# Products with V moved out of the delta-rule recurrence of a hybrid decoder step

## The chip, the core and the metric

The kernel runs on one core of a Trainium2 chip. The metric is device time in microseconds of one execution, the median of the runs. Engines: PE (TensorE) multiplies, PEld is its weight load, DVE (VectorE) and ACT (ScalarE) work elementwise, POOL (GpSimd) too, SP issues DMAs. Each engine takes its instructions in the order in which the program holds them.

## What is computed

One layer over 1024 prompt tokens and 8 x 8 sample tokens, all in float32, D_MODEL 1024. An input projection feeds a short gated convolution and an RWKV-7 head group (8 heads of 64); an output projection, a residual, a squared-ReLU MLP of 4096 and norms follow. The part that the change touches is the state recurrence of each head:

```
def step(s, inp):
    r_t, w_t, k_t, v_t, kk_t, a_t = inp
    s_kk = einsum('bhvk,bhk->bhv', s, kk_t)
    s = s * w_t[:, :, None, :] - s_kk[..., None] * (kk_t * a_t)[:, :, None, :] + v_t[..., None] * k_t[:, :, None, :]
    y_t = einsum('bhvk,bhk->bhv', s, r_t)
    return s, y_t
```

## The kernel before, in words

**Matrix products that fill.** The projections are cut into pieces of 24 matmuls (`fill`, lines L664 and L671, tile `acc`), each matmul 128 x 128 weights against 384, 320 or 256 columns, in the float32r format, three passes over high and low parts. They depend on little and are called fillers here.

**The recurrence.** It runs over chunks of 64 tokens. Heads go in pairs p = 0..3 (head 0 of a pair on partitions 0 to 63, head 1 on 64 to 127), tokens in groups g = 0..2. A unit u = 3p + g has 6, 6 or 4 prompt chunks (64 chunks in all), and the unit g = 2 has one more chunk with the sample tokens (`gen_sample`). For each unit `gen_norms` and `gen_ew` make scaled keys, `gen_tokens` transposes keys and values (KT, VT), masked products land in AMK and AMB (L899, tile `pm`), `gen_invert` solves a 32 x 32 triangular inverse on POOL, `gen_merge` completes it to 64 x 64 on PE (tile `pz`). Then `gen_recur` does per chunk, into one PSUM bank `rc`: KT x V (L1110), AMK x V (L1111), AR x state (L1114), copy to X (L1120, DVE), Tt x X (L1122), scale to UT (L1124, ACT), KT x UT (L1126), and the new state Gh (L1132, DVE), which takes in GD, the decayed old state (L1116, ACT). The weights of these products are 128 x 128, block-diagonal over the two heads, with zeros in the other blocks. The outputs `py` (L1144) are 64 x 64 products, two heads side by side. `gen_finish` normalises py, transposes it (tile `pty`) and gates it.

**What sets the order.** The whole front of the kernel is written by generators; a planner (`Weave.run`) takes from them, one at a time, the step that could start first by its own table of costs, and so writes out the order of every engine once, at build time. A step may need credits (`acq`): PSUM banks by tag (`mm`, `tr`, `rec`, `iv`, `py`), buffers for r, k and v (`xr`, `xk`, `xv`, three each). A filler piece whose result finds no free buffer holds its `mm` bank, and the fillers behind it stand. The order of the projection jobs is the list `main`. After the front, the MLP loop runs in plain program order; the change does not touch it.

Of the kernel before, what the change touches and what calls it, by code (L numbers as in the profile page):

```python
# [28 lines left out]
REC, TR = 2, 2  # L29
# [4 lines left out]
def tile_kernel(ctx: ExitStack, tc: tile.TileContext, io: dict):  # L34
# [227 lines left out]
    class Weave:  # L262
# [47 lines left out]
        def run(self, gens):  # L310

            st = [[0.0, next(g, None), "PE"] for g in gens]
            while any(a is not None for _, a, _ in st):
# [37 lines left out]
                st[i][0] = r if o.get("nb") else t + cost + o.get("lat", self.LAT[eng])  # L351
# [147 lines left out]
    def gen_lora(parts):  # L499

        for p in range(4):
            for g in range(3):
                s, n = GROUPS[g]
                pc = slice(128 * p, 128 * p + 128)
                for nm in parts:
                    x, dst = {"w2": (lw, sig_d), "a2": (la, ta_d), "g2": (None, gate_d)}[nm]
                    m = 3 if x is None else 2
                    yield ck("PE", (n / 2400 + 0.0133) * m, acq=("rec",),
                             deps=[("lw", nm), ("sg" if x is None else "la", g)])
                    pw = ps.tile([128, 512], F32, tag="rec", name="pw", bufs=REC)  # L510
# [12 lines left out]
                    wv.free("rec")  # L523
# [208 lines left out]
    def first(g):  # L732
# [4 lines left out]
    main = (rkv_jobs(0) + conv_jobs(0, "cxb") + conv_jobs(1, "cxb") + rkv_jobs(1) + conv_jobs(2, "cx") + rkv_jobs(2)  # L737
            + conv_jobs(2, "b") + rkv_jobs(3) + conv_jobs(3, "cxb"))
# [4 lines left out]
    def gen_open():  # L743
# [14 lines left out]
        for nm, w, n in (("AR", 192, 3), ("AMK", 192, 3), ("KT", 256, 2)):  # L758
            at[nm + "s"] = [pp.tile([128, 6, w], F32, name=f"{nm}{i}") for i in range(n)]
        load_sgta(0)  # L760
        load_gt(0)
        for i in range(3):
            for h in range(2):
                r, z = slice(64 * h, 64 * h + 64), slice(64 - 64 * h, 128 - 64 * h)
                G.memset(at["ARs"][i][r, :, z], 0.0)
                G.memset(at["AMKs"][i][r, :, z], 0.0)
                if i < 2:
                    G.memset(at["KTs"][i].rearrange("p c (x k) -> p c x k", x=2)[r, :, :, z], 0.0)
# [29 lines left out]
    def gen_norms(u):  # L798
# [8 lines left out]
        yield ck("PE", 0.117 * nch + 0.1, gap=0.1, acq=("tr",), deps=done(u - 3))  # L807
# [18 lines left out]
    def gen_ew(u):  # L826
# [44 lines left out]
        yield ck("DVE", 1.0, deps=done(u - 3) + ([("B", u - 2)] if u > 1 else []))  # L871
# [17 lines left out]
        LT = e["LT"] = at["pp"].tile([128, 6, 64], F32, tag="LT", name="LT", bufs=2)  # L889
        for c0, c1 in ((0, 4), (4, nch)):  # L890
# [9 lines left out]
            for h in range(2):  # L900
# [13 lines left out]
                V.tensor_tensor(x64(AMK, h)[HS[h], c0:c1], pm[0:64],  # L914
# [50 lines left out]
    def gen_tokens(u):  # L965
# [4 lines left out]
        KT = at["KTs"][u % 2].rearrange("p c (x k) -> p c x k", x=2)  # L970
        for c0 in range(0, nch, 3):
# [119 lines left out]

    def gen_recur(u):
# [6 lines left out]
        for c in range(npc):  # L1099
            first = g == 0 and c == 0  # L1100
            yield ck("PE", 0.45, gap=0.02, acq=("rec",), lat=0.2 if first else 0, deps=[("T", u), ("B", u)] + done(u - 1) if c == 0 else [])
            if c == 0:
                AMK, AMB, AR, KT, VT, Tt, dc, nneg = (e[x] for x in ("AMK", "AMB", "AR", "KT", "VT", "Tt", "dc", "nneg"))
# [5 lines left out]
            rc = ps.tile([128, 512], F32, tag="rec", name="rc", bufs=2)  # L1109
            PE.matmul(rc[:, 128:192], KT[:, c, 0, :], VT[:, c, :], start=True, stop=False, skip_group_check=True)  # L1110
            PE.matmul(rc[:, 0:64], AMK[:, c, 0:128], VT[:, c, :], start=False, stop=first, skip_group_check=True)  # L1111
            if not first:
                yield ck("PE", 0.225, gap=0.02, deps=[("G", u, c)] if c else [])
                PE.matmul(rc[:, 0:64], AR[:, c, 0:128], st, start=False, stop=True, skip_group_check=True)  # L1114
                GD = at["pp"].tile([128, 64], F32, tag="GD", name="GD")
                A.activation(GD, st, AF.Copy, scale=dc[:, c:c + 1])  # L1116
                wv.charge("ACT", 0.33)
            yield ck("DVE", 0.2)
            X = at["pp"].tile([128, 64], F32, tag="X", name="X", bufs=1)
            V.tensor_copy(X, rc[:, 0:64])  # L1120
            yield ck("PE", 0.225, gap=0.02)
            PE.matmul(rc[:, 64:128], Tt[:, c, :], X, start=False, stop=True, skip_group_check=True)  # L1122
# [3 lines left out]
            PE.matmul(rc[:, 128:192], KT[:, c, 1, :], UT[:, c, :], start=False, stop=True, skip_group_check=True)  # L1126
            yield ck("DVE", 0.2)
            st = Gh[:, c, :]
            if first:
                V.tensor_scalar(st, rc[:, 128:192], dc[:, c:c + 1], None, op0=ALU.mult)  # L1130
            else:
                V.scalar_tensor_tensor(st, rc[:, 128:192], dc[:, c:c + 1], GD, op0=ALU.mult, op1=ALU.add)  # L1132
            wv.free("rec")
            wv.mark(("G", u, c + 1))
        for c in range(npc):
# [3 lines left out]
            ops = [(AMK[:, c, 128:192], VT[:, c, :]), (AMB[:, c, :], UT[:, c, :])]  # L1139
# [6 lines left out]
        if g == 2:  # L1146
            yield ck("PE", 0.11, acq=("rec",), deps=[("G", u, npc)])
            pt = ps.tile([128, 512], F32, tag="rec", name="ptg", bufs=2)
# [13 lines left out]
    def gen_sample(u):  # L1162
# [22 lines left out]
        wv.free("rec")  # L1185

        yield ck("PE", 0.60, gap=0.08, lat=0.5, acq=("rec",), deps=[("A", u)])
        AMK, AMB, dc, nneg = (e[x] for x in ("AMK", "AMB", "dc", "nneg"))
        px = ps.tile([128, 2, 64], F32, tag="rec", name="pxs", bufs=2)
# [10 lines left out]
        wv.free("rec")  # L1200
        yield ck("PE", 0.45, gap=0.08, acq=("rec",), deps=[("B", u), ("UT", u)])
        Tt, UT = e["Tt"], e["UT"]
        rc = ps.tile([128, 512], F32, tag="rec", name="rcs", bufs=2)
        PE.matmul(rc[:, 0:64], AMK[:, c, 0:128], VT[:, c, :], start=True, stop=False, skip_group_check=True)
        for hc in HS:
            PE.matmul(rc[hc, 0:64], XY[hc, 0, :], ident[hc, hc], start=False, stop=True, skip_group_check=True)
# [7 lines left out]
        wv.free("rec")  # L1214
        yield ck("PE", 0.45, gap=0.1, deps=[("py", u)])
        py = e["py"]
        ops = [(XY[:, 1, :], None), (AMK[:, c, 128:192], VT[:, c, :]), (AMB[:, c, :], UT[:, c, :])]
# [4 lines left out]
        for b0 in range(0, NB, 4):  # L1222
# [6 lines left out]
            yield ck("PE", 0.87, acq=("rec",))  # L1229
            pg = ps.tile([128, 512], F32, tag="rec", name="pgs", bufs=2)  # L1230
            for x in range(2):
                PE.matmul(pg[:, 0:256], KT[:, c, x, :], VM[x].rearrange("p b v -> p (b v)"), start=(x == 0), stop=(x == 1))
# [12 lines left out]
            wv.free("rec")  # L1245
# [12 lines left out]
    def gen_finish(u):  # L1258
# [13 lines left out]
        wv.free("py")  # L1272
# [16 lines left out]
        yield ck("PE", 0.32, acq=("rec",))  # L1289
        pt = ps.tile([128, 512], F32, tag="rec", name="pty", bufs=2)  # L1290
# [6 lines left out]
        wv.free("rec")  # L1297
# [164 lines left out]
    with tc.manual_schedule():  # L1462
# [9 lines left out]
        for i in range(2):  # L1472
            pgs.append(ps.tile([128, 512], F32, tag="rec", name="pg1", bufs=REC))
            PE.matmul(pgs[i], ones, g1[:, 512 * i:512 * i + 512], start=True, stop=True)
        A.copy(g1B[:, :512], pgs[0])
        for t in range(3):
# [6 lines left out]
            if t == 1:  # L1483
# [20 lines left out]
                chain(gen_tokens), chain(gen_bonus),  # L1504
# [177 lines left out]
```

## Time and profile before

| | |
|---|---|
| median of 3 runs | 1469.48 us (1464.67 to 1476.61) |
| the profiled execution | 1467.82 us, span from first to last instruction 1466.1 us |
| PE busy | 1428.1 us, 97% of the span |
| DVE, ACT, POOL busy | 823.6, 508.4, 317.4 us |
| mean granted clock of PE | 0.985 of full speed |

The recurrence lies between about 190 and 615 us. In a timeline the start times of PE's rows follow each other at the pace at which PE takes work; the length of one row is longer than that, since matmuls overlap.

### The profile page before, as it was taken

To read this page: it belongs to the slowest core of one execution; us is meant where nothing else is said; L and a number is where in the kernel's file an instruction comes from. 1 tells how busy PE (TensorE), PEld (TensorE's weight loads), DVE (VectorE), ACT (ScalarE), POOL (GpSimd) and SP (SyncE) were. 2 spreads that over 40 slices of the span, in tenths; PEclk is the share of its full clock that TensorE was granted. 3 is DMA by queue.
4 is the path that set the end of the run, shared out by engine and by line. 5 is a ranking of instruction groups with operands and counts; after the bars stand their busy time and mean duration, and the time that the engine had idled before them with its cause. 6 is when DMAs were issued, how large, how long until landed. Compare 5 with 4: busy or idle time off the path is not lost.

```text
span 1466.1 us, 25883 instructions
## 1 busy us (share of the span) xinstructions
PE 1428.1 (97%) x10163; PEld 1339.9 (91%) x10163; DVE 823.6 (56%) x1788; ACT 508.4 (35%) x1094; POOL 317.4 (22%) x855
## 2 busy tenths in 40 slices
PE   6999999999989997999999999999999999999997
PEld 5999999998989987999999999999999999999996
DVE  6537767787767785666444344444344344444347
ACT  6532334344333432344522332223322332223315
POOL 4011656654665655000000000000000000000004
PEclk8999999999989998999999999999999999999999
DMA  6242332232232325453210111111111111111103
GB/s 193 94 146 87 80 84 69 66 91 57 72 85 57 74 74 184 149 171 101 87 44 29 58 58 44 42 31 59 44 43 30 58 58 44 42 32 58 36 1 122
DMA packets 140228, 108.25 MB, mean 74 GB/s; under 512 B 43837, under 2 KB 131017, under 8 KB 140106
## 3 DMA queue, kind: packets, MB, share of 16 engines
q1 hardware_dynamic: 65322, 61.29, 14.0%
q10 hardware_dynamic: 74784, 45.30, 10.5%
q8 instruction: 80, 1.31, 0.4%
q14 instruction: 42, 0.34, 0.1%
HBM read 88.46 MB, written 18.09 MB: 73 GB/s over the span
## 4 chain that ended last, share of the span: by engine, by line
PE 87%; DVE 5%; DMA 3%; POOL 2%; issue 1%; ACT 1%; SPq 0%; ACTq 0%; POOLq 0%; DVEq 0%
PE acc L103 24%; PE acc L664 21%; PE acc L1547 17%; PE acc L1559 8%; PE acc L671 6%; DMA mr<-mix_d 1%; PE pm L899 1%; PE py L1144 1%; PE pw L516 1%; PE rc L1122 1%; DMA wraw<-in_w_out 1%; PE rc L1111 1%; PE pt L403 1%; POOL wtmp L1040 1%; POOL W L1042 1%
## 5 line engine op out<-in xcount | busy, mean ns | idle before, releaser
L103 PE MATMUL acc<-h_lo,whi 128*128 128x320 f32 (+1 forms) x720 | 234.8, 326 | 0.0
L103 PE MATMUL acc<-h_hi,wlo 128*128 128x320 f32 (+1 forms) x720 | 234.8, 326 | 0.0
L103 PE MATMUL acc<-h_hi,whi 128*128 128x320 f32 (+1 forms) x720 | 234.7, 326 | 0.0
L664 PE MATMUL acc<-h_hi,whi 128*128 128x384 f32 (+1 forms) x672 | 230.5, 343 | 2.8 <-DVE nsT L259 2.8
L664 PE MATMUL acc<-h_lo,whi 128*128 128x384 f32 (+1 forms) x672 | 229.4, 341 | 1.6 <-DVE h_lo L414 1.6
L664 PE MATMUL acc<-h_hi,wlo 128*128 128x384 f32 (+1 forms) x672 | 229.9, 342 | 0.0
L1549 DVE TENSOR_TENSOR x<-acc,x 128x512 f32<-128x512 f32 (+1 forms) x193 | 132.8, 688 | 124.9 <-PE acc L1547 124.9
L1593 POOL TENSOR_TENSOR rsf<-rsf,nhalf 128x1 f32<-128x1 f32 (+1 forms) x9 | 8.0, 888 | 741.5 <-DVE rsf L1590 740.4
L1425 DVE TENSOR_TENSOR slo<-r,shi 128x384 fp32r<-128x384 f32 (+1 forms) x96 | 51.5, 537 | 204.5 <-ACT shi L1423 204.5
L1040 POOL TENSOR_TENSOR wtmp<-W,gM 96x60 f32<-96x60 f32 (+24 forms) x372 | 122.3, 329 | 155.3 <-DMA gM<-lt_d 71.3
L1547 PE MATMUL acc<-f2h,shi 128*128 128x512 f32 (+1 forms) x386 | 150.2, 389 | 0.0
L1547 PE MATMUL acc<-f2h,slo 128*128 128x512 f32 (+1 forms) x386 | 150.0, 389 | 0.0
L1547 PE MATMUL acc<-f2l,shi 128*128 128x512 f32 (+1 forms) x386 | 149.9, 388 | 0.0
L68 ACT CAST f2h<-f2r 128x1024 fp32r<-128x1024 f32 x32 | 32.0, 1047 | 309.1 <-PE acc L1547 309.1
L103 PEld LDWEIGHTS acc<-h_lo,whi 128*128 128x128 f32 x720 | 135.1, 188 | 0.6
L103 PEld LDWEIGHTS acc<-h_hi,whi 128*128 128x128 f32 x720 | 135.1, 188 | 0.6
L103 PEld LDWEIGHTS acc<-h_hi,wlo 128*128 128x128 f32 x720 | 135.2, 188 | 0.0
L664 PEld LDWEIGHTS acc<-h_hi,whi 128*128 128x128 f32 x672 | 128.6, 191 | 4.5 <-ACT KT L981 3.0
L1042 POOL TENSOR_TENSOR W<-W,wtmp 96x60 f32<-96x60 f32 (+24 forms) x372 | 126.3, 340 | 29.2
L664 PEld LDWEIGHTS acc<-h_lo,whi 128*128 128x128 f32 x672 | 128.7, 191 | 2.7 <-DVE h_lo L414 1.9
L664 PEld LDWEIGHTS acc<-h_hi,wlo 128*128 128x128 f32 x672 | 128.6, 191 | 0.4
L1419 ACT ACTIVATE r<-acc 128x384 f32<-128x384 f32 (+1 forms) x96 | 45.3, 472 | 150.9 <-PE acc L103 141.2
(308 smaller groups left out, 2833.2 us busy)
## 6 DMA issues: line engine op xcount, KB each, us to landing
f2r<-in_w_ff SPq DMA_DIRECT2D x32, 512.0 KB
wraw<-in_w_ff ACTq DMA_DIRECT2D x64, 256.0 KB
wraw<-in_w_in ACTq DMA_DIRECT2D x48, 256.0 KB
wraw<-in_w_out ACTq DMA_DIRECT2D x48, 256.0 KB
xt<-in_x_prompt SPq DMA_DIRECT2D x8, 512.0 KB
x<-in_x_prompt SPq DMA_DIRECT2D x8, 512.0 KB
out_y_prompt<-out SPq DMA_DIRECT2D x7, 512.0 KB
gM<-lt_d SPq DMA_DIRECT2D x32, 96.0 KB
```

What stands on the lines that cost most here:

```text
L68: A.copy(hi, src)
L103: PE.matmul(acc[:, :n], a, b, start=(i == 0), stop=(i == 23))
L403: PE.transpose(pt[:, k, :n], xn[:n, 128 * kk:128 * kk + 128], ident[:n, :n])
L664: PE.matmul(acc[:, :n], a, b, start=(k == i == 0), stop=(k == 7 and i == 2))
L671: PE.matmul(acc[:n, :256], a, b, start=(k == i == 0), stop=(k == 7 and i == 2))
L1040: G.tensor_tensor(tv, W[:, 0:nr, r:r + 1].broadcast_to([96, nr, wd]), M[:, r:r + 1, r + 1:32].broadcast_to([96, nr, wd]), op=ALU.mult)
L1042: G.tensor_tensor(W[:, 0:nr, r + 1:32], W[:, 0:nr, r + 1:32], tv, op=ALU.subtract)
L1419: A.activation(r[:, :n], acc[:, :n], AF.Relu)
L1425: V.tensor_tensor(lo, r[:, :n], hi.bitcast(F32), op=ALU.subtract)
L1547: PE.matmul(acc[:, :cn], a, b, start=(j == 0), stop=(j == 3 * FB - 1))
L1549: V.tensor_tensor(x1[t][:, cols], acc[:, :cn], x1[t][:, cols], op=ALU.add)
L1559: PE.matmul(acc[:, :n], a, b, start=(j == 0), stop=(j == 3 * FB - 1))
```

## The change

The two products with V leave the chunk loop. A new generator `gen_kv` makes them for up to three chunks at a time, as 64 x 64 products per head, into a bank of its own; ACT copies AMK x V to KVX[0], DVE writes KT x V times the chunk's decay to KVX[1]. In the chunk loop the DVE step to X adds the KVX value, and GD is a DVE instruction that adds the decayed state to KVX[1]; ACT's GD is gone. AMK and KT lose their zero blocks that only V's products needed. PSUM goes from two `rec` and two `tr` banks to one `rec` and three `tr`; all but the chunk loop and one transpose use `tr`. The transpose at the end of a unit writes into the unit's own `py` bank, which is so held longer. In `gen_sample` the products with `KT` for the new sample states become 64 x 64 too. Some buffers go from 2 to 3 or from 3 to 4, two dependencies are loosened, and the list `main` interleaves the jobs in finer steps.

```diff
-REC, TR = 2, 2
+REC, TR = 1, 3
...
-    main = (rkv_jobs(0) + conv_jobs(0, "cxb") + conv_jobs(1, "cxb") + rkv_jobs(1) + conv_jobs(2, "cx") + rkv_jobs(2)
-            + conv_jobs(2, "b") + rkv_jobs(3) + conv_jobs(3, "cxb"))
+    main = (rkv_jobs(0) + conv_jobs(0, "cxb") + conv_jobs(1, "cx") + rkv_jobs(1) + conv_jobs(1, "b")
+            + conv_jobs(2, "c") + rkv_jobs(2) + conv_jobs(2, "x") + rkv_jobs(3) + conv_jobs(2, "b")
+            + conv_jobs(3, "cxb"))
...
-        for nm, w, n in (("AR", 192, 3), ("AMK", 192, 3), ("KT", 256, 2)):
+        for nm, w, n in (("AR", 192, 3), ("AMK", 128, 3), ("KT", 192, 2)):
...
-        yield ck("DVE", 1.0, deps=done(u - 3) + ([("B", u - 2)] if u > 1 else []))
+        yield ck("DVE", 1.0, deps=done(u - 3))
...
+    def gen_kv(u):
+        p, g = UN[u]
+        e = es[u]
+        npc = 6 if g < 2 else 4
+        for c0 in range(0, npc, 3):
+            cc = range(c0, min(c0 + 3, npc))
+            yield ck("PE", 0.24 * len(cc) + 0.1, gap=0.1, acq=("tr",), deps=[("T", u), ("A", u)] + done(u - 2))
+            if c0 == 0:
+                KVX = e["KVX"] = at["pp"].tile([128, 2, 6, 64], F32, tag="KVX", name="KVX", bufs=2)
+            KT, VT, AMK = e["KT"], e["VT"], e["AMK"]
+            kv = ps.tile([128, 2, 4, 64], F32, tag="tr", name="kv", bufs=TR)
+            for c in cc:
+                for x, w in enumerate((AMK, KT)):
+                    for hs in HS:
+                        PE.matmul(kv[hs, x, c - c0, :], w[hs, c, 0:64], VT[hs, c, :], start=True, stop=True)
+            yield ck("ACT", 0.3, lat=0)
+            A.copy(KVX[:, 0, c0:cc[-1] + 1, :], kv[:, 0, 0:len(cc), :])
+            yield ck("DVE", 0.3)
+            V.tensor_tensor(KVX[:, 1, c0:cc[-1] + 1, :], kv[:, 1, 0:len(cc), :],
+                            e["dc"][:, c0:cc[-1] + 1].unsqueeze(2).broadcast_to([128, len(cc), 64]), op=ALU.mult)
+            wv.free("tr")
+        wv.mark(("KV", u))
...
-            rc = ps.tile([128, 512], F32, tag="rec", name="rc", bufs=2)
-            PE.matmul(rc[:, 128:192], KT[:, c, 0, :], VT[:, c, :], start=True, stop=False, skip_group_check=True)
-            PE.matmul(rc[:, 0:64], AMK[:, c, 0:128], VT[:, c, :], start=False, stop=first, skip_group_check=True)
+            rc = ps.tile([128, 512], F32, tag="rec", name="rc", bufs=REC)
+            X, GD = KVX[:, 0, c, :], KVX[:, 1, c, :]
             if not first:
...
-                GD = at["pp"].tile([128, 64], F32, tag="GD", name="GD")
-                A.activation(GD, st, AF.Copy, scale=dc[:, c:c + 1])
...
-            V.tensor_copy(X, rc[:, 0:64])
+                PE.matmul(rc[:, 0:64], AR[:, c, 0:128], st, start=True, stop=False, skip_group_check=True)
+                yield ck("DVE", 0.2)
+                V.tensor_tensor(X, rc[:, 0:64], X, op=ALU.add)
...
+            if not first:
+                V.scalar_tensor_tensor(GD, st, dc[:, c:c + 1], GD, op0=ALU.mult, op1=ALU.add)
+                wv.charge("DVE", 0.2)
...
-                PE.matmul(pg[:, 0:256], KT[:, c, x, :], VM[x].rearrange("p b v -> p (b v)"), start=(x == 0), stop=(x == 1))
+                for h, hc in enumerate(HS):
+                    k0 = x * (64 + 64 * h)
+                    PE.matmul(pg[hc, 0:256], KT[hc, c, k0:k0 + 64], VM[x][hc].rearrange("p b v -> p (b v)"),
+                              start=(x == 0), stop=(x == 1))
...
-        wv.free("py")
...
-        yield ck("PE", 0.32, acq=("rec",))
-        pt = ps.tile([128, 512], F32, tag="rec", name="pty", bufs=2)
+        yield ck("PE", 0.33)
+        pt = py.rearrange("p c t -> p (c t)")
...
-        wv.free("rec")
+        wv.free("py")
```

On PE, a chunk of unit 5 (the last group of the second pair) reads so before; `rc` is the chunk's bank, `acc` a filler:

```order
L664 MATMUL acc<-h_hi,whi 128x320
L1110 MATMUL rc<-VT,KT_1292 128x64
L1111 MATMUL rc<-VT,AMK_1290 128x64
L1114 MATMUL rc<-Gh,AR_1287 128x64
L664 MATMUL acc<-h_lo,whi 128x320
...
L664 MATMUL acc<-h_hi,whi 128x384
L1122 MATMUL rc<-X,Tt_1284 128x64
```

With the change the first two rows of a chunk are gone from there, and PE visits the new tile `kv` once for up to three chunks, here for unit 0 among fillers:

```order
L664 MATMUL acc<-h_hi,whi 128x320
L1108 MATMUL kv<-VT,AMK_1289 64x64 x2
L1108 MATMUL kv<-VT,KT_1292 64x64 x2
L1108 MATMUL kv<-VT,AMK_1289 64x64 x2
L1108 MATMUL kv<-VT,KT_1292 64x64 x2
L1108 MATMUL kv<-VT,AMK_1289 64x64 x2
L1108 MATMUL kv<-VT,KT_1292 64x64 x2
L664 MATMUL acc<-h_lo,whi 128x320
```

The rows of the chunk loop are so 188 where they were 316, and 128 pairs of 64 x 64 products stand in 24 places. The second place is unit 6, the first of the third head pair. With the change PE's order there has no filler from the unit's first Tt row (L1142) to the end of its sixth chunk; this is its beginning (L1149 is KT x UT, L1138 is AR x state):

```order
L664 MATMUL acc<-h_hi,wlo 128x384
L1142 MATMUL rc<-KVX,Tt_1284 128x64
L977 MATMUL ptk<-ident,KB 128x128 x3
L1149 MATMUL rc<-UT,KT_1292 128x64
L1138 MATMUL rc<-Gh,AR_1286 128x64
L977 MATMUL ptk<-ident,KB 128x128 x3
L1142 MATMUL rc<-KVX,Tt_1284 128x64
L1149 MATMUL rc<-UT,KT_1292 128x64
L1138 MATMUL rc<-Gh,AR_1286 128x64
L993 MATMUL ptv<-ident,xv 64x128 x3
L1142 MATMUL rc<-KVX,Tt_1284 128x64
```

Before, the same unit had one to eight fillers between nearly all of these rows. What stands between the chunk's rows now are the transposes, `kv` and `pm` visits of the units behind it.

## Rows read from the trace of the kernel before

**Rows 1.** The page, busy time of each engine.
```profile
PE 1428.1 (97%) x10163; PEld 1339.9 (91%) x10163; DVE 823.6 (56%) x1788; ACT 508.4 (35%) x1094; POOL 317.4 (22%) x855
```
**Rows 2.** Windows: stretch, length, busy time (instructions) by engine, PEclk, DMA share, GB/s.
```profile
core 0: us, PE busy (x) PEld busy (x) DVE busy (x) ACT busy (x) POOL busy (x), PEclk, DMA share, GB/s
200.00:420.00 220.00, 217.67 (x2176) 200.91 (x2176) 168.09 (x480) 85.66 (x229) 135.43 (x399) 1.00 0.28 71
420.00:450.00 30.00, 26.35 (x257) 23.55 (x256) 17.00 (x50) 9.89 (x28) 19.14 (x56) 0.77 0.25 66
...
553.00:575.00 22.00, 15.43 (x165) 14.04 (x165) 9.67 (x22) 5.41 (x14) 14.95 (x45) 0.77 0.65 210
```
**Rows 3.** Timeline of PE, three products at a chunk's head: start, length, what.
```profile
263.82 0.33 PE L1110 MATMUL rc<-VT,KT 128*128 128x64 f32 x2
263.98 0.39 PE L1111 MATMUL rc<-VT,AMK 128*128 128x64 f32 x2
264.21 0.39 PE L1114 MATMUL rc<-Gh,AR 128*128 128x64 f32 x2
264.40 0.42 PE L664 MATMUL acc<-h_lo,whi 128*128 128x384 f32 x1
264.66 0.33 PE L664 MATMUL acc<-h_hi,wlo 128*128 128x384 f32 x1
```
**Rows 4.** Timeline of PE, one recurrence product between fillers.
```profile
262.54 0.33 PE L1126 MATMUL rc<-UT,KT 128*128 128x64 f32 x2
262.68 0.42 PE L664 MATMUL acc<-h_lo,whi 128*128 128x384 f32 x1
262.94 0.33 PE L664 MATMUL acc<-h_hi,wlo 128*128 128x384 f32 x1
263.11 0.34 PE L664 MATMUL acc<-h_hi,whi 128*128 128x384 f32 x1
```
**Rows 5.** Timeline of PE, a visit of 64 x 64 products between fillers.
```profile
278.15 0.39 PE L664 MATMUL acc<-h_hi,wlo 128*128 128x320 f32 x1
278.47 0.33 PE L1220 MATMUL py<-ident,XY 64*64 64x64 f32 x4
278.64 0.28 PE L1220 MATMUL py<-VT,AMK 64*64 64x64 f32 x4
278.75 0.28 PE L1220 MATMUL py<-UT,AMB 64*64 64x64 f32 x4
278.97 0.41 PE L664 MATMUL acc<-h_hi,whi 128*128 128x320 f32 x1
279.22 0.31 PE L664 MATMUL acc<-h_lo,whi 128*128 128x320 f32 x1
279.36 0.31 PE L664 MATMUL acc<-h_hi,wlo 128*128 128x320 f32 x1
```
**Rows 6.** Timeline of PE, the sample's state products of 256 columns.
```profile
280.39 0.60 PE L1232 MATMUL pgs<-VM,KT 128*128 128x256 f32 x2
280.82 0.59 PE L1232 MATMUL pgs<-Sn,KT 128*128 128x256 f32 x2
```
**Rows 7.** Timeline of PE, a recurrence step with nothing between.
```profile
424.35 0.33 PE L1122 MATMUL rc<-X,Tt 128*128 128x64 f32 x2
425.08 0.43 PE L1126 MATMUL rc<-UT,KT 128*128 128x64 f32 x2 [0.40 <-ACT UT L1124]
```
**Rows 8.** Waits of PE: who, for whom, us in total, times, longest.
```profile
PE rc L1126 <- ACT UT L1124: 4.2, 2, 3.8
PE rc L1122 <- DVE X L1120: 3.2, 6, 1.8
PE acc L664 <- DVE nsT L259: 2.8, 1, 2.8
```
**Rows 9.** Groups by line: busy us, mean ns; idle before, and its end.
```profile
L1116 ACT ACTIVATE GD<-Gh,dc 128x64 f32<-128x64 f32 x60 | 20.8, 346 | 38.9 <-DVE Gh L1132 26.0 <-DMA wraw<-in_w_out 5.7 <-DVE X L1120 3.6
L1124 ACT ACTIVATE UT<-rc,nneg 128x64 f32<-128x64 f32 x64 | 20.0, 312 | 72.3 <-PE rc L1122 69.9 <-DMA wraw<-in_w_in 2.3
L1132 DVE SCALAR_TENSOR_TENSOR Gh<-rc,dc,GD 128x64 f32<-128x64 f32 x60 | 16.8, 281 | 18.9 <-PE rc L1126 17.7
L1120 DVE COPY X<-rc 128x64 f32<-128x64 f32 x64 | 14.1, 221 | 9.8 <-PE rc L1114 8.4 <-PE rc L1111 0.3
```
**Rows 10.** Windows: the whole recurrence, columns as in the second group.
```profile
200.00:560.00 360.00, 351.15 (x3538) 323.28 (x3537) 273.59 (x772) 138.91 (x377) 216.35 (x626) 0.98 0.28 71
```

More of the change, by code (lines that the diff above doesn't have):

```diff
@@ L888, in gen_ew @@
         AMB = e["AMB"] = at["pp"].tile([128, 6, 64], F32, tag="AMB", name="AMB", bufs=3)
-        LT = e["LT"] = at["pp"].tile([128, 6, 64], F32, tag="LT", name="LT", bufs=2)
+        LT = e["LT"] = at["pp"].tile([128, 6, 64], F32, tag="LT", name="LT", bufs=3)
         for c0, c1 in ((0, 4), (4, nch)):
@@ L1125, in gen_recur @@
             yield ck("PE", 0.225, gap=0.02)
-            PE.matmul(rc[:, 128:192], KT[:, c, 1, :], UT[:, c, :], start=False, stop=True, skip_group_check=True)
+            PE.matmul(rc[:, 128:192], KT[:, c, 64:192], UT[:, c, :], start=False, stop=True, skip_group_check=True)
             yield ck("DVE", 0.2)
             st = Gh[:, c, :]
[L1129 to L1132, printed above, removed]
+            V.scalar_tensor_tensor(st, rc[:, 128:192], dc[:, c:c + 1], GD, op0=ALU.mult, op1=ALU.add)
             wv.free("rec")
@@ L1147, in gen_recur @@
             yield ck("PE", 0.11, acq=("rec",), deps=[("G", u, npc)])
-            pt = ps.tile([128, 512], F32, tag="rec", name="ptg", bufs=2)
+            pt = ps.tile([128, 512], F32, tag="rec", name="ptg", bufs=REC)
             PE.transpose(pt[0:64, 0:128], st, ident)
@@ L1184, in gen_sample @@
         V.tensor_copy(G0, pt)
-        wv.free("rec")
-        yield ck("PE", 0.60, gap=0.08, lat=0.5, acq=("rec",), deps=[("A", u)])
+        wv.free("tr")
+        yield ck("PE", 0.60, gap=0.08, lat=0.5, acq=("tr",), deps=[("A", u)])
         AMK, AMB, dc, nneg = (e[x] for x in ("AMK", "AMB", "dc", "nneg"))
-        px = ps.tile([128, 2, 64], F32, tag="rec", name="pxs", bufs=2)
+        px = ps.tile([128, 2, 64], F32, tag="tr", name="pxs", bufs=TR)
         for b in range(NB):
@@ L1199, in gen_sample @@
         V.tensor_copy(XY[:, 0:2, :], px)
-        wv.free("rec")
-        yield ck("PE", 0.45, gap=0.08, acq=("rec",), deps=[("B", u), ("UT", u)])
+        wv.free("tr")
+        yield ck("PE", 0.45, gap=0.08, acq=("tr",), deps=[("B", u), ("UT", u)])
         Tt, UT = e["Tt"], e["UT"]
-        rc = ps.tile([128, 512], F32, tag="rec", name="rcs", bufs=2)
-        PE.matmul(rc[:, 0:64], AMK[:, c, 0:128], VT[:, c, :], start=True, stop=False, skip_group_check=True)
+        rc = ps.tile([128, 512], F32, tag="tr", name="rcs", bufs=TR)
         for hc in HS:
-            PE.matmul(rc[hc, 0:64], XY[hc, 0, :], ident[hc, hc], start=False, stop=True, skip_group_check=True)
+            PE.matmul(rc[hc, 0:64], AMK[hc, c, 0:64], VT[hc, c, :], start=True, stop=False)
+        for hc in HS:
+            PE.matmul(rc[hc, 0:64], XY[hc, 0, :], ident[hc, hc], start=False, stop=True)
         yield ck("DVE", 0.2)
@@ L1236, in gen_sample @@
                             op=ALU.mult)
-            wv.free("rec")
-            yield ck("PE", 0.43, acq=("rec",))
-            pt = ps.tile([128, 4, 128], F32, tag="rec", name="pto", bufs=2)
+            wv.free("tr")
+            yield ck("PE", 0.43, acq=("tr",))
+            pt = ps.tile([128, 4, 128], F32, tag="tr", name="pto", bufs=TR)
             for b in range(4):
@@ L1244, in gen_sample @@
             A.copy(So, pt[0:64])
-            wv.free("rec")
+            wv.free("tr")
             wv.defer(lambda So=So, b0=b0: store_s(So, b0))
@@ L1472, in tile_kernel @@
         for i in range(2):
-            pgs.append(ps.tile([128, 512], F32, tag="rec", name="pg1", bufs=REC))
+            pgs.append(ps.tile([128, 512], F32, tag="tr", name="pg1", bufs=TR))
             PE.matmul(pgs[i], ones, g1[:, 512 * i:512 * i + 512], start=True, stop=True)
@@ L1503, in tile_kernel @@
                 chain(gen_ew),
-                chain(gen_tokens), chain(gen_bonus),
+                chain(gen_tokens), chain(gen_kv), chain(gen_bonus),
                 gen_open(), gen_rows(), gen_mixed(),
```

54 lines of the change are left out of this document (25 added, 29 removed).

## The prediction

> **What bounds the kernel now.** I read the page's busy times first: PE is busy for 1428.1 of 1466.1 us [rows 1], so the time is what PE has to do plus 38.0 us in which it stands. Less work elsewhere is worth only as much as it shortens those stands; more work on PE costs its full length. Then the windows: from 200 to 420 us PE stands for 2.3 of 220 us at the full clock [rows 2], so there the recurrence is covered by fillers and any saved PE slot is a gain. Two stretches are not covered: 420 to 450 us stands for 3.65 us and runs its 26.35 busy us at 0.77 of the full clock, and 553 to 575 us stands for 6.57 us and runs 15.43 us at 0.77 [rows 2]. Counting (1 - 0.77) of the busy time as lost, they cost 3.65 + 6.1 = 9.7 us and 6.57 + 3.5 = 10.1 us. These 20 us are what a better order could free in the recurrence. The waits name what ended them: a UT on ACT, one X on DVE, and in the first stretch a filler that waited 2.8 us for the evacuation of an earlier one [rows 8].
>
> **The change part by part.** The sum is made against the profiled execution, 1467.8 us, which is 1.7 us under the median of the runs.
>
> *V's products leave the loop.* PE's price of an instruction is the distance of starts, since rows overlap. The three products at a chunk's head: from 263.82 to the second filler at 264.66 is 0.84 us, less one filler slot of 0.17 makes 0.67 [rows 3]. One product alone: 262.54 to 262.94, less 0.17 (262.94 to 263.11), is 0.23 [rows 4]. Two of three products fewer are so 0.44 us a chunk; 64 chunks give **-28.2 us**.
>
> *They come back as 64 x 64 products.* The trace has no `kv`, but it has the same shape in the sample's outputs, three head pairs between fillers: 278.15 to 279.22 is 1.07 us, less two filler slots of 0.14 (279.22 to 279.36) leaves 0.79 [rows 5]. The pairs follow each other in 0.11 to 0.12 us (278.64 to 278.75), so three are 0.35; the other 0.43 belongs to the visit, however many pairs it holds: 0.17 us ahead of the first pair, the rest behind. The change has 128 chunk-wise pairs (two per chunk, 0.117 each: 15.0 us) in 24 visits (10.3 us): **+25.3 us**. At the cheaper end the visits cost nothing, at the dearer end 0.43; I take 0.43, the row of the same shape. Where a visit stands in a stretch in which PE waits anyway, it is hidden; the order shows two `kv` visits in unit 6 like that, -0.9.
>
> The Trainium skill (TensorEngine Tiling (Array Packing), Key Properties) says that changing the tiling mode, not just the tile, drains TensorE. It speaks against this change, and the 0.43 us of a visit agree. The same page's Theoretical Speedup allows up to a factor of two for a small dimension; by that alone, without the drains, the move would gain 28.2 - 15.0 = 13.2 us and the time be about 1455, an estimate.
>
> *The sample's state products.* Two products of 256 columns follow at 0.43 us [rows 6], 0.86 per visit, 8 visits. As 64 x 64 two heads stand side by side. If the narrow form streams twice as fast, a visit saves 0.43; if each pair takes 0.43 like the wide one, it adds a visit's 0.43. That is -3.4 to +3.4. The narrow pairs seen run at 0.117 for 64 columns [rows 5], four times which is 0.47, near the wide product, so I take **+3.4**. The narrow form in the sample's own X product saves about 0.1 four times, -0.4.
>
> PE's work together: -28.2 + 25.3 - 0.9 + 3.4 - 0.4 = **-0.8 us**, between -14 and 0.
>
> *ACT and DVE.* ACT loses GD, 60 times 0.346 = 20.8 us, and gets 24 copies of about a UT's 0.31, 7.5 us [rows 9]. It is off the path. DVE gets GD in the form of Gh, 60 x 0.281 = 16.9 us; KVX, 24 times at least 0.28 and at most three times that, taken at 0.35, 8.4 us; X as an addition rather than a copy, 64 x (0.281 - 0.221) = 3.8 us [rows 9]. From 200 to 560 us DVE was busy for 273.6 of 360 us, 76% [rows 10]; with 29 more it is 84%. The cover is the fillers between two products of a chunk. A step needs 0.73 us from start to start when nothing is between [rows 7]; four fillers and the product itself give 4 x 0.17 + 0.23 = 0.91, so 0.18 us to spare. I cost DVE's load at nothing, with the rival below if that cover does not hold.
>
> *The new order.* Counting the order's rows between the 188 products of the chunk loop, priced at the paces above, before had 5 steps with less PE work than 0.7 us, short by 2 us in all; the change has 22, short by 8.4. Thirteen of them (5.2 us) are unit 6, whose six chunks have no filler. There the fillers stand for r, k and v buffers that the units behind must free; that is also what the 2.8 us wait at 430 us was [rows 8], so I hold unit 6 for that stretch's successor: the 9.7 us go and 5.2 us come, with a clock as in the other uncovered stretch, 15 us at 0.77 or 3.5 us. Net -1.0. The other nine steps (unit 10 above all) add 3.1 - 2 = +1. At 553 to 575 us UT stood behind ACT's DMA issues of output weights and mix rows; the order still has that burst between two UT of unit 10, so the 10.1 us stay.
>
> *At no cost:* `tr` with three banks in place of two and two; the transpose in the `py` bank, which makes the next unit's outputs wait for the normalisation of the last, with 26 and 52 fillers ahead in the longest cases; fewer memsets on POOL; deeper small buffers. The MLP behind 640 us keeps its order.
>
> Sum: -0.8 - 1.0 + 1.0 = -0.8, so **1467 us**, no change. A measurement of this kernel can tell about 1% from no change: faster is under 1455, slower over 1484.
>
> **The rivals.**
>
> 1. *Forecast, chance 0.48:* the products' saving is eaten by the visits, one uncovered stretch replaces the other. Its own range is 1456 to 1478.
>
> 2. *The visits are cheap and the stretch at 420 us leaves no successor, 0.28.* For it: ACT is relieved by 13 us, the chain of a chunk is 0.44 us shorter at its head, and a visit next to another narrow one shares its 0.43. Against: the order puts nearly all 24 between fillers or full-width products. PE's work then falls by 13 and the stretch gives back up to 9.7 less unit 6's 5.2, together 17.7: 1450 us. The same rule of Theoretical Speedup without drains is a part of this case.
>
> 3. *DVE takes the bound in the recurrence, slower, 0.16.* The place is Gh and X: DVE works in order, GD now stands ahead of Gh, and every chunk's spare is 0.18 us against GD's 0.28. If GD, KVX and the 0.5 us elementwise instructions keep DVE behind PE's order, each of 60 chunks loses between 0.10 and 0.28 us, 6 to 17 us, and unit 6's steps, with DVE between all of them, 5 more: up to 1467 + 22 = 1489. It decides once DVE is busy for over nine tenths of 40 us stretches; 84% on the mean speaks against it, and so does the fact that DVE's X cost only 3.2 us of wait before [rows 8].
>
> 4. *The change does not free PE because unit 6 costs more than its count, 0.08.* With six chunks at 0.73 us for each of three steps and more behind late transposes, the low clock holds for 30 us: 0.5 x 20 us more than counted, 1477.
>
> **Numbers.** The time is the likeliest case's. The range 1446 to 1486 takes in rival 2 with its bounds, and most of rival 3. Faster by over 1% has 0.28 of rival 2 and a little of the forecast's edge; slower has most of rival 3 and the edge of rival 4; the rest is no change.
>
> **What would show it.** `kv` visits: the distance from the filler ahead to the second filler behind, 1.13 us above filler slots if I am right, 0.70 if the visits are free. `pgs`: 1.29 or 0.43. PE's busy time within 5 us of 1428, with fewer us of `rc`. Unit 6: its six chunks in 15 us, PE standing for 5 us, a granted clock under 1. The stretch with the 2.8 us wait gone from where it was. DVE busy by 25 to 30 us more, and PE's wait for X and Gh still under 6 us. I would be wrong if PE's busy time fell by 10 us or more, or if waits for DVE took over 10 us outside unit 6.

## The result, and the profile after

The changed kernel takes 1482.0 us (median of 12 runs, 1477.4 to 1486.0), the kernel before 1469.4 in the same rounds: ratio 1.0076, 95% interval 1.0057 to 1.0095. It is slower by 12.6 us, inside the range of the prediction and off its forecast of no change. The profiled execution has a span of 1480.0 us, 13.9 more than before. The page of the changed kernel, to be read beside [rows 1]:

```profile
PE 1430.4 (97%) x10459; PEld 1329.1 (90%) x10459; DVE 839.2 (57%) x1868; ACT 498.3 (34%) x1058; POOL 315.6 (21%) x849
```

PE is busy 2.3 us longer and stands 49.6 us rather than 38.0. So 11.6 of the 13.9 us are standing. The waits of PE say for whom (us in total, times, longest), and so do those of ACT and of SyncE's DMA queue:

```profile
PE rc L1149 <- ACT UT L1147: 22.0, 6, 12.3
...
PE rc L1138 <- DVE Gh L1152: 2.1, 6, 0.4
PE rc L1142 <- DVE KVX L1140: 0.9, 3, 0.4
```
```profile
ACT UT L1147 <- DMA w_d<-W: 21.6, 2, 15.5
```
```profile
SPq L1049 <- POOL W L1043: 99.8, 11, 23.6
```

One wait for UT of 12.3 us is new; before, the two waits for UT made 4.2 us together [rows 8]. The windows place it (columns as in [rows 2]):

```profile
core 0: us, PE busy (x) PEld busy (x) DVE busy (x) ACT busy (x) POOL busy (x), PEclk, DMA share, GB/s
185.00:190.00 5.00, 3.99 (x24) 3.36 (x22) 2.89 (x10) 0.31 (x1) 4.14 (x12) 1.00 0.14 42
190.00:195.00 5.00, 0.00 (x0) 0.00 (x0) 0.00 (x0) 0.00 (x0) 3.90 (x15) 0.74 0.00 0
195.00:200.00 5.00, 0.00 (x0) 0.00 (x0) 0.00 (x0) 0.00 (x0) 2.51 (x11) 0.50 0.03 5
200.00:205.00 5.00, 3.71 (x13) 3.71 (x14) 1.37 (x5) 0.90 (x2) 0.00 (x0) 0.50 0.52 132
...
355.00:365.00 10.00, 6.72 (x30) 6.41 (x30) 3.26 (x9) 1.83 (x4) 1.54 (x3) 0.83 0.31 74
420.00:445.00 25.00, 22.19 (x165) 17.69 (x165) 15.74 (x50) 7.11 (x22) 10.42 (x31) 0.59 0.16 34
...
553.00:575.00 22.00, 21.72 (x283) 19.36 (x281) 17.25 (x44) 11.18 (x31) 13.78 (x35) 1.00 0.15 33
575.00:595.00 20.00, 13.48 (x147) 12.42 (x148) 6.81 (x20) 3.82 (x9) 8.16 (x29) 0.66 0.79 256
```

From 190 to 200 us no engine works but POOL, which inverts. PE comes back at the lower clock level (0.50, 1.2 GHz). The timelines of ACT with its DMA queue, of SyncE's queue and of PE (start, length, what, and in brackets the idle time and its end):

```profile
185.06 0.31 ACT L1147 ACTIVATE UT<-rc,nneg 128x64 f32<-128x64 f32 x1 [0.97 <-PE rc L1142]
200.49 0.38 ACTq L640 DMA_DIRECT2D wraw<-in_w_in  x1
200.92 0.31 ACT L1147 ACTIVATE UT<-rc,nneg 128x64 f32<-128x64 f32 x1 [15.54 <-DMA w_d<-W]
```
```profile
174.20 0.43 SPq L1012 DMA_DIRECT2D W<-unit_d  x1
198.32 3.25 SPq L1049 DMA_DIRECT2D w_d<-W  x4
```
```profile
187.94 0.33 PE L1142 MATMUL rc<-KVX,Tt 128*128 128x64 f32 x2
...
201.29 0.69 PE L1149 MATMUL rc<-UT,KT 128*128 128x64 f32 x2 [12.27 <-ACT UT L1147]
...
359.13 0.43 PE L1149 MATMUL rc<-UT,KT 128*128 128x64 f32 x2 [3.28 <-ACT UT L1147]
```

UT of chunk 2 of unit 0 was ready for ACT at 188.3 us, when PE had its product. But ahead of it in ACT's order stands a weight load, and its issue came at 200.49, two microseconds after SyncE issued the store of unit 1's inverse (`w_d`), which had waited for POOL's inversion from 174.6 to 198.3. The built order shows why a load of weights waits for that store. Both name one DMA semaphore (first ACT's rows, then SyncE's; "waits" are the semaphores):

```
171 L1147 ACTIVATE UT<-rc,nneg 128x64 [waits PE_49]
172 L640 DMA wraw<-in_w_in 128x4x128 [waits DMAHW1_49,DVE_49]
173 L1147 ACTIVATE UT<-rc,nneg 128x64 [waits PE_49]

106 L1049 DMA w_d<-W 192x1x32 [waits DMAHW1_49,Pool_49]
```

The transfers of SyncE and ACT take eight such semaphores in turn, and here the load comes eight transfers after the store, so it waits until the store has landed. The chain is POOL, store, semaphore, weight load, UT, PE. The inversion itself was not late: it ended 10 us earlier than in the kernel before, at 198.3 rather than 208.8. The same chain strikes a second time, more briefly: of ACT's two waits of 21.6 us for `w_d`, the second is 6.1 us, and PE stands for 3.28 of them, until 359 us.

The new stage's price stands in PE's timeline (one visit of three chunks, and one of the sample's state products):

```profile
132.38 0.31 PE L664 MATMUL acc<-h_hi,whi 128*128 128x320 f32 x1
132.62 0.33 PE L1108 MATMUL kv<-VT,AMK 64*64 64x64 f32 x4
132.79 0.28 PE L1108 MATMUL kv<-VT,KT 64*64 64x64 f32 x4
...
133.47 0.42 PE L664 MATMUL acc<-h_lo,whi 128*128 128x320 f32 x1
133.72 0.31 PE L664 MATMUL acc<-h_hi,wlo 128*128 128x320 f32 x1
...
284.80 0.31 PE L664 MATMUL acc<-h_hi,whi 128*128 128x320 f32 x1
285.04 0.65 PE L1255 MATMUL pgs<-VM,KT 64*64 64x256 f32 x4
285.52 0.60 PE L1255 MATMUL pgs<-Sn,KT 64*64 64x256 f32 x4
286.05 0.41 PE L664 MATMUL acc<-h_lo,whi 128*128 128x320 f32 x1
286.30 0.30 PE L664 MATMUL acc<-h_hi,wlo 128*128 128x320 f32 x1
```

Measured as in [rows 5], a visit takes 133.72 - 132.38 - 2 x 0.145 = 1.05 us (the five visits that stand between fillers: 1.04 to 1.06), and the state products 286.30 - 284.80 - 0.29 = 1.21, against 1.13 and 1.29 in the prediction.

### The profile page after: what moved, and what is told of

The parts are those of the page before. It is cut to its first block, busy times and chain, and to the rows that moved or that the text cites. A ratio compares the mean times of both kernels' runs of the same rounds, so it can differ in the third digit from the quotient of the medians.

```text
span 1480.0 us, 26558 instructions
## 1 busy us (share of the span) xinstructions
PE 1430.4 (97%) x10459; PEld 1329.1 (90%) x10459; DVE 839.2 (57%) x1868; ACT 498.3 (34%) x1058; POOL 315.6 (21%) x849
## 4 chain that ended last, share of the span: by engine, by line
PE 82%; POOL 6%; DVE 4%; DMA 2%; issue 2%; ACT 1%; SPq 1%; ACTq 0%; POOLq 0%; DVEq 0%
PE acc L103 24%; PE acc L1570 17%; PE acc L664 16%; PE acc L1582 8%; PE acc L671 7%; POOL W L1043 3%; POOL wtmp L1041 3%; PE py L1164 2%; PE pm L899 1%; PE pw L516 1%; PE rc L1142 1%; PE rc L1149 1%; PE kv L1108 1%; PE rc L1138 1%; DMA gM<-lt_d 1%
```

## The experiments

Theory A is the chain above; B is a dearer price of the visits; C the unfilled stretch of unit 6 with its clock; D VectorE's load. Each ratio is to the kernel before, timed on the same chip.

**The one load on SyncE.** Its place there is ahead of the store; PE's order is untouched.

```diff
-                (SP if x < 2 else A).dma_start(raw, src)
+                (SP if x < 2 or (x, i) == (12, 0) else A).dma_start(raw, src)
```

> One weight load, the one that ScalarE issues between the scaling UT of chunk 1 and that of chunk 2 of unit 0, is issued by SyncE instead, where it stands ahead of the store of unit 1's inverse; TensorE's order is that of the changed kernel, instruction by instruction. Theory A (the loss is the 12.3 us stall at 189 us: ScalarE holds UT behind the issue of that load, and the issue waits for the store, which waits for GpSimd's inversion): no TensorE wait over 3 us between 180 and 215 us, about 12.3 us of idle time and some 3 us of halved clock come back, 1466 to 1470 against 1482. Theory B (the 64x64 visits cost more than the products they replace): TensorE's work is untouched, 1480 to 1484. Theory C (the stretch of unit 6 without fillers and its low clock make the loss): 1480 to 1484. Theory D (VectorE's and ScalarE's longer steps): 1480 to 1484.

1470.25 us, ratio 0.9992 (0.9979 to 1.0006). One transfer on another queue takes the loss away: the ratio was 1.0076. The window that held the stall:

```profile
180.00:215.00 35.00, 32.71 (x331) 30.95 (x330) 18.08 (x59) 11.61 (x31) 22.25 (x67) 1.00 0.24 62
```

UT of chunk 2 now runs at 188.82, while the store still waits until 199.35. The orders on all engines but the two queues are those of the changed kernel. B, C and D fall as the cause of the loss; A is shown.

**Paced inversions.**

```diff
-        yield ck("DVE", 1.0, deps=done(u - 3))
+        yield ck("DVE", 1.0, deps=done(u - 3) + ([("B", u - 2)] if u > 1 else []))
-        LT = ... name="LT", bufs=3)
+        LT = ... name="LT", bufs=2)
```

> The changed kernel with one loosening taken back: the steps AR and LT of a unit wait again for the merged inverse of two units before, and LT has two buffers again. The plan then spaces the inversions, and the load after the second UT no longer follows the store of unit 1's inverse on the same semaphore. Theory A: no stall at 189 us, and none over 4 us in 100 to 420 us; 1464 to 1471. Theories B and C: 1479 to 1484 (visits and the order of jobs are the same). Theory D: 1478 to 1484.

1474.8 us, ratio 1.0031 (1.0020 to 1.0041): above what A expected. The stall at 189 us went, and another of the same making came at 525 us, behind a row load. PE, ACT and SyncE there:

```profile
536.62 0.48 PE L1108 MATMUL kv<-VT,AMK 64*64 64x64 f32 x4 [11.10 <-DVE KVX L1112]
```
```profile
534.59 1.22 ACTq L1344 DMA_DIRECT2D mr<-mix_d  x2
535.85 0.32 ACT L1110 COPY KVX<-kv 128x192 f32<-128x192 f32 x1 [15.61 <-DMA w_d<-W]
```
```profile
532.42 3.36 SPq L1049 DMA_DIRECT2D w_d<-W  x4
```

The chain of A returns with another victim: ACT's copy of the new stage, then DVE, then PE. The spacing does not cure it; it only chooses which transfer falls behind the store.

**The jobs of before**, and **the planner's price of an inversion step** (`0.5 + ...` to `0.63 + ...`), each alone in the changed kernel.

> The changed kernel with the list of jobs of the kernel before. Theory A: the load that followed the store on its semaphore now falls elsewhere, no stall at 189 us; the stretch that unit 6 had without fillers goes to another place as it did before, and the 420 to 450 us stretch loses about 10 us to idle time and clock as before; 1465 to 1472. Theory C: the loss of the stretch of unit 6 (some 12 us of idle time and half clock) falls to the 10 us of before, so 1478 to 1482. Theories B and D: 1480 to 1484.

> The changed kernel with the planner's price of a step of the inversion raised from 0.5 + ... to 0.63 + ..., so that an inversion is planned at about the 25 us that the trace shows instead of 21.4. Nothing else is edited, but the whole order moves with it. Theory A: loads and stores are planned where they happen, no TensorE wait over 4 us behind a weight load in 100 to 420 us, UT's wait falls from 22 us to under 8; 1462 to 1470. Theories B, C and D: 1478 to 1486.

1497.7 us, ratio 1.0189 (1.0161 to 1.0216), and 1483.6, ratio 1.0087 (1.0071 to 1.0103). Both miss A's figures, and C's 1478 to 1482 is missed too: the 12 us stall is gone in both, and the new orders lose as much or more elsewhere. With the old jobs PE is busy for 58.73 of 70 us from 400 us on and 56.28 of 70 from 545; with the other price 51.48 of 65 from 530, at 0.68 of the clock. Both edits move the whole order, so neither run tells what its edit alone is worth.

**The stores by GpSimd**, which computes what they store; the orders on PE, DVE and ACT stay.

```diff
-            SP.dma_start(w_d[:nb].rearrange("b (m q) t -> q b m t", q=4)[q], ...
+            G.dma_start(w_d[:nb].rearrange("b (m q) t -> q b m t", q=4)[q], ...
```

> The changed kernel with the four stores of each unit's inverse issued by GpSimd, which computes them, instead of SyncE. The orders on TensorE, VectorE and ScalarE stay those of the changed kernel. Theory A (a weight load and the store share a semaphore, so ScalarE's queue stands behind GpSimd's inversion): SyncE's queue and the loads no longer wait for an inversion, no TensorE wait over 3 us from 180 to 215 us; 1464 to 1472, with 1470 as in the run with the load on SyncE. If GpSimd's own issue of a store is slow (no row shows it), the inversions come later by that, unit after unit, and UT's other waits grow: 1472 to 1480. If the shared semaphore was not the cause: 1480 to 1484.

1470.55 us, ratio 0.9999 (0.9978 to 1.0020): a second way to cut the chain, and the same time as the first. From 40 to 400 us PE stands for 1.2 us; the second stand of that chain is gone too.

**Both of the last kind together**: paced inversions, stores by GpSimd.

> The run with the paced inversions (1474.8) with the stores of the inverses issued by GpSimd as well. There ScalarE stood 15.6 us at 520 to 536 us behind a row load that waited for such a store, and TensorE 11.1 us for it. Theory A: that stall goes too, with its clock some 13 us: 1460 to 1466, below the kernel before. If the stall there had another cause: 1472 to 1478.

1467.96 us, ratio 0.9997 (0.9978 to 1.0017), 2 us above the expected range. The 11.1 us stall at 525 us is gone; but from 535 to 600 us PE is busy for 53.43 of 65 us at 0.84 of the clock, where ACT waits for row loads and holds a cast and UT behind them.

**The new jobs in the kernel before.**

> The kernel before with the new list of jobs alone, nothing else of the change. If the finer list is worth something in itself (the old list in the changed kernel cost 16 us against the new one), 1455 to 1465. If it only serves a recurrence whose steps have less TensorE work of their own, the kernel before moves within 1%: 1465 to 1476. Slower, 1476 to 1490, if its loads fall behind stores in new places.

1486.2 us, ratio 1.0110 (1.0090 to 1.0130). The list is no gain in itself: with either kernel, the other kernel's list is slower. PE's idle time and clock were lost in several places, with no single wait over 4 us; which rows make it is open.

**Two products back into each step**, on the kernel with the load on SyncE.

```diff
+                for x in range(2):
+                    PE.matmul(rc[:, 192 + 64 * x:256 + 64 * x], AR[:, c, 0:128], st, ...
```

> The run with the load on SyncE (1470.25) with two products of 128x128 by 128x64 put into each of the 60 recurrence steps that have a state, into columns that nothing reads. It leaves nothing out of the computation. At 0.22 us each they are 120 x 0.22 = 26.4 us. If TensorE's work counts one for one: 1494 to 1499. If the steps of the stretches without fillers (unit 6, units 10 and 11, about 14 steps) take them in their waits, 14 x 0.44 = 6 us less: 1488 to 1494. If the products' removal was worth little since the recurrence is bound by its waits: 1470 to 1485.

1488.4 us, ratio 1.0117 (1.0090 to 1.0145), against 0.9992 without them: 18 us, at the lower edge of the middle case. Between fillers they cost what the prediction took for those removed:

```profile
184.77 0.33 PE L1138 MATMUL rc<-Gh,AR 128*128 128x64 f32 x2
184.93 0.61 PE L1140 MATMUL rc<-Gh,AR 128*128 128x64 f32 x4
185.35 0.42 PE L664 MATMUL acc<-h_hi,wlo 128*128 128x384 f32 x1
185.61 0.33 PE L664 MATMUL acc<-h_hi,whi 128*128 128x384 f32 x1
```

185.61 - 184.77 - 0.17 = 0.67 for three, 0.23 for one [rows 4], so 0.44 for two. Of 60 x 0.44 = 26.4 us, 8 did not show: PE's idle time from 40 to 660 us fell from 17.1 to 8.4 us, while what it lost to the clock, counted as in the table below, rose from 16.7 to 20.3. Work in a loop step is worth its length only where the step is covered.

**The price of the stage**, on the kernel with stores by GpSimd: each product twice, and one visit per chunk.

```diff
-                    for hs in HS:
+                    for hs in HS + HS:
```
```diff
-        for c0 in range(0, npc, 3):
-            cc = range(c0, min(c0 + 3, npc))
+        for c0 in range(npc):
+            cc = range(c0, c0 + 1)
```

> The run with the stores by GpSimd (1470.55), with every 64x64 product of the new stage issued twice into the same place (the second overwrites the first with the same value; nothing is left out). The visits stay 24, the pairs grow by 128. By the prediction's price of a pair, 0.117 us: 128 x 0.117 = 15.0, 1484 to 1488. If a pair costs less inside a visit and the visit's fixed part more: 1476 to 1483. If the stage lies in stretches where TensorE waits anyway: 1470 to 1475.

> The run with the stores by GpSimd, with the new stage visited once per chunk instead of once per three: 64 visits instead of 24, the same 128 pairs, and 40 more copies on each of ScalarE and VectorE. The prediction's price of a visit, 0.43 us: 40 x 0.43 = 17.2, 1485 to 1491. By the cheaper row, 0.33: 13.2, 1482 to 1486. If entering the 64x64 form costs little: 1470 to 1476. A load that falls behind another wait in the new order may add 5 to 15 us, to be told from the trace.

1479.8 us, ratio 1.0078 (1.0050 to 1.0105), and 1489.1, ratio 1.0135 (1.0100 to 1.0170). The first is 11.6 us longer by the ratios (0.9999 without the doubling) where 15 were expected; the intervals of the two ratios leave room for 15, and PE's work, counted as in the table below, is 13.6 us more. Its time lies in the case of cheaper pairs, which the visits below do not bear out. The second is in the range for a visit of 0.43 us, but by luck: a visit costs less, and a 5.6 us wait for UT at 198 us is in it. The visits themselves can be read exactly. With the products doubled:

```profile
133.29 0.31 PE L664 MATMUL acc<-h_hi,whi 128*128 128x320 f32 x1
133.53 0.45 PE L1108 MATMUL kv<-VT,AMK 64*64 64x64 f32 x8
...
135.08 0.42 PE L664 MATMUL acc<-h_lo,whi 128*128 128x320 f32 x1
135.33 0.31 PE L664 MATMUL acc<-h_hi,wlo 128*128 128x320 f32 x1
```

One chunk a visit:

```profile
133.14 0.31 PE L664 MATMUL acc<-h_hi,whi 128*128 128x320 f32 x1
133.38 0.33 PE L1108 MATMUL kv<-VT,AMK 64*64 64x64 f32 x4
133.55 0.28 PE L1108 MATMUL kv<-VT,KT 64*64 64x64 f32 x4
133.76 0.42 PE L664 MATMUL acc<-h_lo,whi 128*128 128x320 f32 x1
134.01 0.31 PE L664 MATMUL acc<-h_hi,wlo 128*128 128x320 f32 x1
```

12 pairs take 1.75 us, 6 take 1.05, 2 take 0.58: a pair costs 0.70 / 6 = 0.117, and a visit 1.05 - 0.70 = 0.35 whatever it holds. Full-width products have no such part (0.67 for three, 0.23 for one). The Trainium skill (TensorEngine Tiling (Array Packing), Key Properties) names a drain at a change of the tiling mode and does not price it; a cost for each visit agrees with it, though no run here shows the drain itself.

**Rows by SyncE; UT by VectorE**, each on the kernel with paced inversions and stores by GpSimd.

```diff
-        A.dma_start(raw[:, :n], mix_d[128 * k:128 * k + 128, s:s + n])
+        SP.dma_start(raw[:, :n], mix_d[128 * k:128 * k + 128, s:s + n])
```
```diff
-            A.activation(UT[:, c, :], rc[:, 64:128], AF.Copy, scale=nneg[:, c:c + 1])
+            V.tensor_scalar(UT[:, c, :], rc[:, 64:128], nneg[:, c:c + 1], None, op0=ALU.mult)
```

> The run with paced inversions and stores by GpSimd (1467.96), with the row loads of the output projection issued by SyncE instead of ScalarE. TensorE's order is the same. ScalarE stood 4.4 us before a row's cast behind such a load at 574 to 580 us, TensorE 4.2 us for it, and 2.5 us at 561 us. If ScalarE's queue is what holds them: 1460 to 1465. If the rows come no earlier on SyncE's queue: 1466 to 1472.

> The run with paced inversions and stores by GpSimd (1467.96), with the 64 scalings UT made by VectorE instead of ScalarE, and planned so. If the recurrence's waits come from ScalarE's queue (TensorE waited 3.7 us for UT there, and the stretches of units 6, 10 and 11 cost some 5, 12 and 8 us of idle time and half clock): a shorter step and no UT behind a load, 1455 to 1464. If VectorE takes the wait over (64 x 0.25 = 16 us more on it): 1468 to 1480. The order moves with it, so a load may fall behind another wait.

1459.6 us, ratio 0.9925 (0.9896 to 0.9954): faster than both kernels. From 535 to 600 us PE is busy for 61.69 us, not 53.43; the orders on PE, DVE and POOL are the same, so the row loads in ACT's order are what held it. UT on VectorE gives 1472.4, ratio 1.0025 (1.0005 to 1.0045): no gain, though PE then waits for no UT longer than 0.6 us. The row loads still hold ACT there (9.1 us ahead of four casts from 535 to 600 us), and the whole order was planned anew, so that run does not tell what UT's place in ACT's order costs.

**The same queues for all three**: the kernel before, the changed one, and the changed one with paced inversions, each with stores by GpSimd and rows by SyncE, on one chip.

> The kernel before, with the two queue edits that gave 1459.6 on the changed kernel: stores of the inverses by GpSimd, row loads of the output projection by SyncE. TensorE's order is that of the kernel before. If the gain of that run belongs to the V-product stage once the queues are clear (TensorE's work fell by some 3.4 us, and the waits it was lost to are gone): the kernel before has no UT behind a store to lose, 1464 to 1470. If the gain belongs to the queues alone: 1458 to 1463, the same as the changed kernel with them.

> The changed kernel with the same two queue edits and its own inversions, not paced; TensorE's order is that of the changed kernel. Against 1470.55 with the stores by GpSimd alone, where the stretch of units 10 and 11 lost 15 us to idle time and half clock. If ScalarE's queue makes that stretch, some 5 to 8 us come back: 1460 to 1466. If not: 1468 to 1472.

> The fastest version so far (changed kernel, paced inversions, stores by GpSimd, row loads by SyncE) timed again beside the two others on one chip: 1457 to 1463. If the pacing of the inversions is what it gains against the version with the same queues and no pacing, it is 2 to 6 us below that one; if not, they agree within 2 us.

1459.2 us, ratio 0.9927 (0.9902 to 0.9953); 1462.3, ratio 0.9943 (0.9922 to 0.9965); 1460.0, ratio 0.9928 (0.9903 to 0.9952). The gain belongs to the queues; which of the two edits gives it to the kernel before, no run tells. With them the change of this case gains nothing: the changed kernel is 3.1 us above the kernel before, and 0.8 with the pacing, which is within the intervals. The pacing makes 2.3 us by the medians, the lower edge of what was expected of it. Where the saved work goes is seen in the stretches of unit 6 and of unit 10, here of the kernel before with these queues:

```profile
400.00:445.00 45.00, 40.79 (x430) 37.07 (x430) 33.06 (x94) 18.22 (x50) 35.56 (x103) 0.96 0.30 79
545.00:570.00 25.00, 20.91 (x244) 19.61 (x244) 14.56 (x34) 8.47 (x20) 17.52 (x46) 0.86 0.67 217
```

and of the changed kernel with them, not paced:

```profile
400.00:445.00 45.00, 41.04 (x402) 33.79 (x398) 34.36 (x105) 17.45 (x50) 23.08 (x59) 0.85 0.26 63
545.00:570.00 25.00, 22.40 (x201) 19.91 (x202) 16.43 (x44) 8.71 (x22) 20.64 (x57) 0.80 0.50 162
```

PE stands no longer, but does fewer products (402 for 430, 201 for 244) at a lower clock. Idle time and clock loss, added over windows of 5 us from 40 to 660 us (length less busy time, and busy time times one less the clock):

| kernel | span | idle | clock | span less both |
|---|---|---|---|---|
| before | 1466.1 | 16.0 | 10.1 | 1440.0 |
| changed | 1480.0 | 27.0 | 17.6 | 1435.4 |
| changed, the load on SyncE | 1470.5 | 17.1 | 16.7 | 1436.7 |
| before, new queues | 1454.2 | 12.4 | 3.7 | 1438.1 |
| changed, new queues | 1457.8 | 8.3 | 12.4 | 1437.1 |
| changed, new queues, paced | 1458.3 | 9.4 | 14.4 | 1434.5 |

The last column, PE's work at full clock, falls by 1.0 to 4.6 us with the change where the queues are the same. It differs by 1.9 between the two runs of the kernel before, which have one order on PE, so it is good to about 2 us. The clock column, 7 to 11 us more with the same queues, takes the fall back. Whether the clock falls for want of the products that left or by the new order, which leaves unit 6 without fillers, is not shown: with two products put back into each step it lost more, not less (20.3 for 16.7).

## Why the prediction was wrong, step by step

**What bounds the kernel** held: the loss is PE's standing, 11.6 us of 13.9. That PE's busy time stayed within 5 us of 1428, as foretold, is in part luck: by the table, 7.5 us of lower clock stand in it against 4.6 us of saved work.

**PE's work** held in its mechanism. V's products: 0.44 us a chunk, as taken and as measured when two were put back. The visit was mis-sized by a fifth, 0.35 for 0.43; 24 x 0.35 + 128 x 0.117 = 23.3 us rather than 25.3. State products: 1.21 - 0.86 = 0.35, times 8 is 2.8 rather than 3.4. The two visits taken as hidden, which no run shows by themselves, are then 0.7. The sum is -28.2 + 23.3 - 0.7 + 2.8 - 0.4 = -3.2 us for -0.8, and the table's last column agrees within its 2 us. The Trainium skill's rule (TensorEngine Tiling (Array Packing), Theoretical Speedup), taken without the drains, left PE 13.2 us less. The pairs agree with it (0.117 us for 0.22); the visits, 24 x 0.35 = 8.4 us, speak against leaving the drains out.

**ACT and DVE at nothing** held. PE waited 3.0 us for X and Gh together, under the 6 named. DVE's busy time rose by 15.6 us, about half of the 25 to 30 foretold; from 200 to 560 us it hardly moved, 274.2 us for [rows 10].

**The new order, taken at -1.0 + 1.0 and so at nothing, is the step that failed.** It counted PE's rows between two products and never followed ACT's and SyncE's queues past POOL's store, although the change let the inversions run earlier and so moved stores and loads against each other. The 12.3 us of standing and 1.9 of half clock behind it (3.71 x 0.5 from 200 to 205 us) were in no term, nor were the 3.3 us of the second such stand. With the one load on another queue the loss is gone. The data were there: UT behind ACT's issues was named for 553 to 575 us, as a burst that stays, and not looked for elsewhere.

Within that step, unit 6 was forecast at 5.2 + 3.5 us; it stands 2.8 and loses 22.19 x 0.41 = 9.1 to the clock. The 2.8 us wait of [rows 8] went, as foretold. The burst of unit 10 stayed, as foretold, only later: 553 to 575 us is full, and 575 to 595 us loses 6.5 + 4.6 = 11.1 us, for the 10.1 of before. ACT issues the same four weights and two rows between two UT, and PE waits for a UT behind them, first before and then after:

```profile
556.88 2.00 ACTq L640 DMA_DIRECT2D wraw<-in_w_out  x4
563.96 0.69 PE L1126 MATMUL rc<-UT,KT 128*128 128x64 f32 x2 [3.84 <-ACT UT L1124]
```
```profile
574.24 2.18 ACTq L640 DMA_DIRECT2D wraw<-in_w_out  x4
586.53 0.69 PE L1149 MATMUL rc<-UT,KT 128*128 128x64 f32 x2 [4.30 <-ACT UT L1147]
```

**The rivals.** The second (cheap visits, no successor) did not come: the visits cost 0.35 and unit 6 is the successor. The third, VectorE, named the right side with the wrong engine. The fourth was right that unit 6 costs more than its count and that the clock is most of it, but not in size: 11.9 us measured for that stretch, 8.7 counted, where it asked for 10 more. Without the stall the kernel stands at 1470, so it helps to explain why nothing is gained, not the loss. That 1482.0 lies inside the range of 1446 to 1486 is luck: its upper end was there for the third rival.

## What to carry to other kernels

When a change moves work on one engine, follow every transfer issue that stands in the order of an engine on the critical chain, and ask what that issue waits for, a shared semaphore included; a store that waits for a slow engine should be issued by that engine or by a queue that nothing on the chain needs. Before a faster variant is credited to its arithmetic, give the old kernel the same queues. Do not count work taken out of stretches that are not covered as gained: here the waiting or a lower clock took it back.

## What the hardware showed

- Between full-width products, a visit to the 64x64 form costs 0.35 us and 0.117 us for a pair of 64 columns; a full-width product of 64 columns costs 0.22. At 256 columns a pair costs (1.21 - 0.35) / 2 = 0.43 us, an estimate with the same 0.35 for the visit, just what the full-width product of 256 columns does [rows 6].
- After 12.3 us without work PE ran at 1.2 GHz from 201 to past 205 us, and the clock of unit 6's stretch fell to 0.59 with PE busy for 22.19 of 25 us by the rows.
- Transfers issued by GpSimd cost it 0.66 us each (the row of the group in the run with the stores there), and that run takes the same time as the one with the load on SyncE, 1470.55 and 1470.25 us:

```profile
L1049 POOL DMA_DIRECT2D w_d<-W x48 | 30.6, 662 | 2.7 <-POOL W L1043 2.7
```
